# A hybrid diffusion trunk on one core: an output projection over eight full blocks, a fused split of the weights, and unread products in the mixing

## The chip, the core and the metric

The kernel runs on one core of one Trainium2 chip, as one program. The metric is the device time of an execution in microseconds (us), lower is better. Engines are named as in the profile: PE is TensorE's matmul side (PEld its weight loads), DVE is VectorE, ACT is ScalarE, POOL is GpSimd, and SP is the sync engine, whose queue issues all of this kernel's DMAs.

## The reference, cut to what matters

A trunk of two layers runs over 128 context tokens and 256 latent tokens; they are one stream of T = 384 columns, of width 1024. Each layer is a half-step SwiGLU, a token mixing, and a second half-step SwiGLU, each behind an RMS norm with shift, scale and gate from a conditioning vector.

The token mixing projects its input once and runs three head groups side by side:

```
out_a = gqa_attention(a_q, keys_a, vals_a)             # 6 heads of 64: width 384
out_b = rms_norm(gla_bidir(...)) * silu(b_r)           # 4 heads of 64: width 256
out_c = rms_norm(diff_attention(c_q, keys_c, vals_c))  # 4 heads of 96: width 384
out   = concatenate([out_a, out_b, out_c]) @ w_out     # 1024 x 1024
```

Latent tokens read latent and context keys, context tokens only context keys. diff_attention takes the difference of two softmaxes in each head. gla_bidir is linear attention with decays, in both directions. Everything is fp32.

## The kernel before, in words

**Layout.** Activations lie transposed: 128 features on the partitions, the 384 tokens in the columns. A product with a weight is three matmuls (`mm3`): weight and activation are each split into a rounded high part and the rest, and high x high, high x low and low x high are summed in a PSUM bank. `load_split` (L297 to L305) loads a weight tile into one of five raw buffers, rounds it on ACT (L303) and subtracts on DVE (L304); three buffers each for the high and the low part. PE executes its matmuls in the order of its queue.

**Stages.** `ffn` runs 22 blocks of gate and up, then 8 output tiles; beside them, `AdaStream` computes the conditioning vectors with DVE (L254). `mixing` runs named stages in an order written out by hand for each layer (`ORDER`): `wq`, `wk`, `wa`, `wv` and `bv` are projections (`proj_m`), `rq`, `rk` and `ra` norm, rotate and transpose queries and keys on PE, `L0` to `L6` are the levels of the linear attention (in each, `scores` computes 24 small products of 32 rows by 64 columns), `c0` to `c3` are the four differential heads (`c_head`: scores, two softmaxes, transposes, values, sum of squares), `n0` and `n1` norm two heads each, `s0` and `s1` split them, `p0` to `p2` and `o0` to `o2` are the other attention, `go` ends the linear attention. A scheduler interleaves stages on the engines where data and buffers allow, so instructions of several stages alternate in the trace.

**Products in fp32.** Those outside `mm3` (scores, values, sums of squares) take both operands in fp32; the trace shows each as two matmul passes. Transposes are one pass each.

**The output projection** at the end of `mixing` runs over 8 output tiles. The mixed features come in nine blocks, in the order `KORD`: three of the `a` group and two of the `b` group with 128 rows each, and four of the `c` group with 96 rows each, one for every head. The weight `wo` of a tile is loaded in two parts, of five and four blocks; the 96-row blocks are padded to 128 in memory.

**PSUM.** Three banks `mm`, three `ax`, and the banks `ada` and `both` that stages take in turn.

Of the kernel before, what the change touches and what calls it, by code (L numbers as in the profile page):

```python
# [17 lines left out]
P = 128  # L18
D = 1024
KT = 8  # L20
# [42 lines left out]
ORDER = (  # L63
    ("ha br bq hb bk wq bv lg rq de wk st L0 rk L1 cx wa wv L2 c0 L3 c1 L4 c2 ra L5 L6 n0 s0 c3 n1 p0 ax "
     "s1 go o0 p1 p2 o1 o2").split(),
    ("br ha hb bq bk bv lg L0 wq rq wk de L1 st rk L2 wa cx wv L3 c0 ra L4 c1 c2 L5 c3 n0 L6 p0 ax "
     "go o0 p1 s0 p2 o1 n1 s1 o2").split(),
)
KORD = (
    ("c0 c1 c2 c3 b0 b1 a0 a1 a2").split(),  # L70
    ("a0 b0 b1 c0 c1 a1 c2 c3 a2").split(),
)
# [9 lines left out]
def _build(ctx, tc, nc, I, O):  # L82
# [214 lines left out]
    def load_split(src, cols=WCOL):  # L297
        raw = wp.tile([P, WCOL], F32, tag="wraw", bufs=NRAW, name="wraw")
        di = nc.sync.dma_start(out=raw[:, :cols] if len(src.shape) == 2 else
                               raw[:, :cols].rearrange("p (j c) -> p j c", j=src.shape[1]), in_=src)  # L300
        hi = wp.tile([P, WCOL], F32R, tag="whi", bufs=3, name="whi")
        lo = wp.tile([P, WCOL], F32R, tag="wlo", bufs=3, name="wlo")
        S.activation(out=hi[:, :cols], in_=raw[:, :cols], func=AF.Copy)  # L303
        vi = V.tensor_tensor(out=lo[:, :cols], in0=raw[:, :cols], in1=hi[:, :cols].bitcast(F32), op=ALU.subtract)  # L304
        return hi, lo, vi, di  # L305

    def mm3(ps, lh, ll, rh, rl, start, stop):
        PE.matmul(ps, lhsT=lh, rhs=rh, start=start, stop=False)  # L308
        PE.matmul(ps, lhsT=lh, rhs=rl, start=False, stop=False)  # L309
        return PE.matmul(ps, lhsT=ll, rhs=rh, start=False, stop=stop)  # L310

    def newton(pool, ss, n, scale, parts, tag):
# [248 lines left out]
    def mixing(l, us, acc, nxt):  # L561
        turn["own"] = {"mm": ("both",), "ax": ("ada",)}
        r_ = make_rstd(acc)
        with tc.tile_pool(name=f"mix{l}", bufs=1) as mp:
# [3 lines left out]
            def t512(n=512):  # L568
                return mt([P, 512], "t5", N512)[:, :n]


            kta = mt([P, T], "kta")
# [36 lines left out]
            def proj_m(name, n, kper):  # L609
                ps = [mmps()[:, :n] for _ in range(3)]  # L610
# [126 lines left out]
            def a_probs(i):  # L737

                pts = [mt([P, 3, LAT], "pt", NPT), mt([P, 3, LAT], *(("e", 3) if i else ("pt", NPT)))]
                for t in range(2):  # L740
                    pp = [mmps()[:, :T] for _ in range(2)]
                    for g in range(2):
                        r = slice(64 * g, 64 * g + 64)
                        PE.matmul(pp[g], lhsT=qta[r, i, (t + 1) * P:(t + 2) * P], rhs=kta[r, :], start=True, stop=True)
                    for g, (p, rs) in enumerate(map(smax, pp)):
                        S.activation(out=p, in_=p, func=AF.Copy, scale=rs)
                        to_pt(p.rearrange("p (a b) -> p a b", a=3), 3, pts[g][:, :, t * P:(t + 1) * P])
                return pts

            def a_out(i, pts):  # L750
# [12 lines left out]
                V.tensor_tensor(out=lo, in0=po, in1=hi.bitcast(F32), op=ALU.subtract)  # L763
                moa.append((P, hi, lo))

# [17 lines left out]
            def c_head(h, oc, osq, pss):  # L783
                pt = mt([P, 3, LAT], "pt", NPT)
                for t in range(2):
                    pp = [(mmps if PMM[4] else axps)()[:, :T] for _ in range(2)]
                    for m in range(2):
                        r = slice(64 * m, 64 * m + 64)
                        PE.matmul(pp[m], lhsT=qtc[r, h, (t + 1) * P:(t + 2) * P], rhs=ktc[r, h, 0:T],  # L789
                                  start=True, stop=True)  # L790
                    (p0, r0), (p1, r1) = map(smax, pp)
# [20 lines left out]
            def c_first(j):  # L812
                cp[j] = mt([P, 2, T], "oc", 2)[:96], mt([P, 2, T], "pt", NPT)[:96], []
                c_next(j, 0)

            def c_next(j, i):
                oc, osq, pss = cp[j]
                c_head(2 * j + i, oc[:, i, :], osq[:, i, :], pss)

            def c_norm(j):  # L820
                oc, osq, pss = cp[j]
                r = rsq_bcast(mp, pss, T, 1.0 / 96, 96, "c", osq, osq)
                V.scalar_tensor_tensor(out=oc, in0=oc, scalar=gco[:96], in1=r, op0=ALU.mult, op1=ALU.mult)

            def c_split(j):
                oc = cp[j][0]
                for i in range(2):
                    hi = hp.tile([P, TW], F32R, tag="h", name="chi")[:96, :T]
                    S.activation(out=hi, in_=oc[:, i, :], func=AF.Copy)
                    lo = hp.tile([P, TW], F32R, tag="h", name="clo")[:96, :T]  # L830
                    V.tensor_tensor(out=lo, in0=oc[:, i, :], in1=hi.bitcast(F32), op=ALU.subtract)
                    moc.append((96, hi, lo))

# [60 lines left out]

            def scores(q, k, h, cross):
                ps = (mmps if PMM[10] else axps)()[:, :192].rearrange("p (c t) -> p c t", c=3)
                r = slice(32 * h, 32 * h + 32)
                for c in range(3):
                    for f in range(2):
                        fq = 1 - f if cross else f  # L900
                        PE.matmul(ps[64 * f:64 * f + 64, c, :], lhsT=k[r, c * P + 64 * f:c * P + 64 * f + 64],  # L901
                                  rhs=q[r, c * P + 64 * fq:c * P + 64 * fq + 64], start=True, stop=True)
                return ps

            def gla_diag():
                for h in range(4):
                    ps = scores(qk[:, 0, :], qk[:, 1, :], h, False)
                    V.tensor_tensor(out=sd[h // 2][:, h % 2], in0=ps, in1=two_i[:, None, :].to_broadcast([P, 3, 64]),
                                    op=ALU.mult)

            def gla_level(li):
# [33 lines left out]
            def gla_out():  # L945
# [31 lines left out]
                for i in range(2):  # L977
# [3 lines left out]
                    V.tensor_tensor(out=lo, in0=ot[:, i, :], in1=hi.bitcast(F32), op=ALU.subtract)  # L981
                    mob.append((P, hi, lo))

            sv = {}

# [4 lines left out]
            def a_rope():  # L990
                xa, ra = sv["a"]
                for t in range(3):
# [28 lines left out]
            def c_rope(w):  # L1021
                xc, rc = sv[w]
                for t in range(3):
# [9 lines left out]
                    ps = (mmps if PMM[13] else axps)()  # L1033
                    for h in range(4):
                        PE.transpose(ps[:, h * P:(h + 1) * P], pad[:, 2 * h:2 * h + 2, :].rearrange("p a b -> p (a b)"),
# [33 lines left out]
            turn["own"] = {"mm": ("both",), "ax": ()}  # L1069
            mo = [{"a": moa, "b": mob, "c": moc}[n[0]][int(n[1])] for n in KORD[l]]  # L1070
            acc = new_acc()
            us = []
            for m in range(KT):
                ps = mmps()[:, :T]
                for k0, k1 in ((0, 5), (5, 9)):
                    w = load_split(I["wo"][l, m][:, k0 * P:k1 * P], (k1 - k0) * P)
                    for k in range(k0, k1):
                        c = (k - k0) * P
                        n, hi, lo = mo[k]
                        mm3(ps, w[0][:n, c:c + P], w[1][:n, c:c + P], hi, lo, k == 0, k == 8)  # L1080
                end_tile(l, 1, m, ps, acc, nxt, None)
# [137 lines left out]
```

## Time and profile before

| what | value |
|---|---|
| median of three runs | 1598.27 us (1590.26 to 1601.04) |
| profiled execution, its own time | 1599.75 us |
| its span, first to last instruction | 1597.9 us |
| PE busy | 1563.3 us (98%) |
| DVE busy | 1229.3 us (77%) |
| ACT busy | 738.8 us (46%) |
| mean granted clock of TensorE | 0.980 |

A row of a window gives each engine's busy time in that stretch with the number of its instructions, then the granted clock as a share of the full one, the DMA engines' share and what they moved. Durations of single matmuls overlap, since they are pipelined: the distance between the starts of two is the pace. A bracket at the end of a timeline row is the idle time before the instruction and who ended it.

### The profile page before, as it was taken

What the parts mean: (1) busy time and instruction counts of PE and PEld (TensorE: products, weight loads), DVE (VectorE), ACT (ScalarE), POOL (GpSimd) and SP (SyncE); (2) the same over time, 40 slices, a digit from 0 to 9 for tenths busy, and PEclk for the clock granted to TensorE, in tenths of its full rate; (3) what the DMA queues carried; (4) which work ended last, traced back from release to release, by engine and by line L of the source; (5) the groups of instructions that cost most, each with busy time, mean ns of one, the idle gap of its engine ahead of it and who ended that gap; (6) DMA issues with size and microseconds to landing.
All of it is one profiled execution on the core that took longest, in us unless ns stands there. A gap on an engine that the chain in (4) does not pass through costs nothing.

```text
span 1597.9 us, 25055 instructions
## 1 busy us (share of the span) xinstructions
PE 1563.3 (98%) x9370; PEld 1464.0 (92%) x9370; DVE 1229.3 (77%) x2294; ACT 738.8 (46%) x1444; POOL 196.2 (12%) x239
## 2 busy tenths in 40 slices
PE   7999999999999999999999999999999999999999
PEld 5999999997558999999999999999875699999999
DVE  4799999888766888898968889667787767666532
ACT  4544433365466544443344444335546754444321
POOL 1211130030000211111001111102000011111100
PEclk9999999999789999999999999999898999999999
DMA  9677778542104566666666666543321064443441
GB/s 330 231 229 229 226 225 261 165 122 83 45 1 140 168 197 202 201 192 207 204 213 197 210 197 195 174 144 96 113 77 39 1 230 144 143 137 130 120 143 57
DMA packets 83230, 256.38 MB, mean 160 GB/s; under 512 B 10978, under 2 KB 19746, under 8 KB 82722
## 3 DMA queue, kind: packets, MB, share of 16 engines
q1 hardware_dynamic: 83108, 254.78, 50.3%
q8 instruction: 74, 1.21, 0.3%
q14 instruction: 48, 0.39, 0.1%
HBM read 251.99 MB, written 2.75 MB: 159 GB/s over the span
## 4 chain that ended last, share of the span: by engine, by line
PE 90%; DVE 6%; ACT 2%; issue 1%; DMA 1%; POOL 1%; SPq 0%; DVEq 0%; ACTq 0%; POOLq 0%
PE mm L308 20%; PE mm L310 20%; PE mm L309 20%; PE both L308 7%; PE both L309 7%; PE both L310 7%; PE mm L789 1%; DVE wlo L304 1%; PE ax L803 1%; PE ax L901 1%; PE ax L721 1%; DVE junk L254 1%; PE ax L807 0%; DVE ht L397 0%; PE ax L758 0%
## 5 line engine op out<-in xcount | busy, mean ns | idle before, releaser
L303 ACT ACTIVATE whi<-wraw 128x1024 fp32r<-128x1024 f32 (+4 forms) x358 | 348.4, 975 | 461.2 <-PE mm L309 259.1
L304 DVE TENSOR_TENSOR wlo<-wraw,whi 128x1024 fp32r<-128x1024 f32 (+4 forms) x358 | 451.8, 1264 | 131.0 <-ACT whi L303 129.0
L310 PE MATMUL mm<-h,wlo 128*128 128x386 f32 x1096 | 373.3, 341 | 2.5 <-DVE wlo L304 2.5
L308 PE MATMUL mm<-h,whi 128*128 128x386 f32 x1096 | 372.8, 341 | 2.6 <-POOL h L367 1.4
L309 PE MATMUL mm<-h,whi 128*128 128x386 f32 x1096 | 372.5, 340 | 0.0
L254 DVE SCALAR_TENSOR_TENSOR junk<-araw,cb 128x1024 f32<-128x1024 f32 x256 | 312.3, 1220 | 0.8
L310 PEld LDWEIGHTS mm<-h,wlo 128*128 128x128 f32 x1096 | 208.0, 190 | 4.2 <-DVE wlo L304 3.5
L308 PEld LDWEIGHTS mm<-h,whi 128*128 128x128 f32 x1096 | 207.6, 190 | 4.6 <-ACT whi L303 1.7
L309 PEld LDWEIGHTS mm<-h,whi 128*128 128x128 f32 x1096 | 207.6, 189 | 1.6 <-issue 0.7
L477 POOL TENSOR_TENSOR alo<-s,ahi 128x384 fp32r<-128x384 f32 x88 | 115.5, 1314 | 641.5 <-ACT ahi L475 614.9
L309 PE MATMUL mm<-alo,whi 128*128 128x384 f32 x528 | 177.9, 337 | 0.0
L310 PE MATMUL mm<-ahi,wlo 128*128 128x384 f32 x528 | 177.9, 337 | 0.0
L308 PE MATMUL mm<-ahi,whi 128*128 128x384 f32 x528 | 177.9, 337 | 0.0
L308 PE MATMUL both<-h,whi 128*128 128x386 f32 x360 | 122.5, 340 | 0.0
L309 PE MATMUL both<-h,whi 128*128 128x386 f32 x360 | 122.1, 339 | 0.0
L310 PE MATMUL both<-h,wlo 128*128 128x386 f32 x360 | 122.0, 339 | 0.0
L475 ACT ACTIVATE ahi<-s 128x384 fp32r<-128x384 f32 x88 | 46.3, 526 | 129.4 <-DVE s L472 129.3
L309 PEld LDWEIGHTS mm<-alo,whi 128*128 128x128 f32 x528 | 99.2, 188 | 0.0
L310 PEld LDWEIGHTS mm<-ahi,wlo 128*128 128x128 f32 x528 | 99.2, 188 | 0.0
L308 PEld LDWEIGHTS mm<-ahi,whi 128*128 128x128 f32 x528 | 99.2, 188 | 0.0
L469 DVE TENSOR_TENSOR u<-mm,rstd 128x384 f32<-128x384 f32 x66 | 36.6, 554 | 60.8 <-PE mm L310 60.8
L467 ACT ACTIVATE s<-s,bc 128x128 f32<-128x128 f32 (+1 forms) x176 | 70.7, 449 | 8.0 <-ACT bc L418 0.7
(365 smaller groups left out, 2446.7 us busy)
## 6 DMA issues: line engine op xcount, KB each, us to landing
wraw<-in_wgu SPq DMA_DIRECT2D x170, 512.0 KB, 4.2
araw<-in_w_adat SPq DMA_DIRECT2D x128, 512.0 KB, 4.0
wraw<-in_wd SPq DMA_DIRECT2D x64, 512.0 KB, 4.2
wraw<-in_wd SPq DMA_DIRECT2D x32, 384.0 KB, 3.5
araw<-in_w SPq DMA_DIRECT2D x16, 512.0 KB, 5.6
wraw<-in_wo SPq DMA_DIRECT2D x16, 320.0 KB, 3.0
wraw<-in_wit SPq DMA_DIRECT2D x8, 512.0 KB, 3.4
wraw<-in_wa SPq DMA_DIRECT2D x8, 512.0 KB, 3.6
```

Source lines behind the costliest of these rows:

```text
L254: V.scalar_tensor_tensor(out=junk, in0=w, scalar=1.0, in1=self.cb[:, c, :], op0=ALU.mult, op1=ALU.mult, accum_out=self.acc[:, f, c:c + 1])
L303: S.activation(out=hi[:, :cols], in_=raw[:, :cols], func=AF.Copy)
L304: vi = V.tensor_tensor(out=lo[:, :cols], in0=raw[:, :cols], in1=hi[:, :cols].bitcast(F32), op=ALU.subtract)
L308: PE.matmul(ps, lhsT=lh, rhs=rh, start=start, stop=False)
L309: PE.matmul(ps, lhsT=lh, rhs=rl, start=False, stop=False)
L310: return PE.matmul(ps, lhsT=ll, rhs=rh, start=False, stop=stop)
L467: S.activation(out=s[:, a:b], in_=s[:, a:b], func=AF.Silu, bias=bg[:, c:c + 1])
L469: vi = V.tensor_tensor(out=u, in0=pu[:, :T], in1=r, op=ALU.mult)
L475: S.activation(out=hi, in_=s, func=AF.Copy)
L477: G.tensor_tensor(out=lo, in0=s, in1=hi.bitcast(F32), op=ALU.subtract)
L721: pi = PE.transpose(ps[:, i * P:(i + 1) * P], p[:, i, :], ident)
L789: PE.matmul(pp[m], lhsT=qtc[r, h, (t + 1) * P:(t + 2) * P], rhs=ktc[r, h, 0:T], start=True, stop=True)
```

## The change

**The output projection over eight blocks.** Head 3 of the `c` group has no block of its own any more. Its 96 rows fill the rows 96 to 127 of the blocks of heads 0, 1 and 2, 32 rows each, so that eight blocks have 128 rows. `c_norm(1)` writes these rows with three instructions of 32 rows; `c_split(0)` now needs `c_norm(1)`, and `ORDER` moves `s0` behind `n1` in layer 0 and `n1` forward in layer 1. Each part of `wo` has four blocks; the part with the head blocks is loaded by three DMAs (rows 0 to 95, the gathered rows, and the last rows of the one other block).

**The low part of a weight** is computed by `scalar_tensor_tensor` (times 1.0, minus the high part) instead of `tensor_tensor`, on the same operands.

**33 unread products in each mixing.** `warm` issues n products of a 128 x 128 matrix of ones with the identity, in fp32, into columns of a PSUM bank that nobody reads: 4 ahead of the first `proj_m`, 8 ahead of the scores of head 0, one behind the scores of every second head in `gla_diag` and the levels 0 to 2 (8), one ahead of each group of transposes in `a_rope` and `c_rope` (9), 4 ahead of the output projection. The scores of the `a` group and of the other `c` heads get none.

```diff
-    ("ha br bq hb bk wq bv lg rq de wk st L0 rk L1 cx wa wv L2 c0 L3 c1 L4 c2 ra L5 L6 n0 s0 c3 n1 p0 ax "
-     "s1 go o0 p1 p2 o1 o2").split(),
+    ("ha br bq hb bk wq bv lg rq de wk st L0 rk L1 cx wa wv L2 c0 L3 c1 L4 c2 ra L5 L6 n0 c3 n1 p0 ax "
+     "s0 s1 go o0 p1 p2 o1 o2").split(),
...
-     "go o0 p1 s0 p2 o1 n1 s1 o2").split(),
+     "go n1 o0 p1 s0 p2 s1 o1 o2").split(),
...
-    ("c0 c1 c2 c3 b0 b1 a0 a1 a2").split(),
-    ("a0 b0 b1 c0 c1 a1 c2 c3 a2").split(),
+    ("c0 c1 c2 b0 b1 a0 a1 a2 c3").split(),
+    ("a0 b0 b1 a1 c0 c1 c2 a2 c3").split(),
...
-        vi = V.tensor_tensor(out=lo[:, :cols], in0=raw[:, :cols], in1=hi[:, :cols].bitcast(F32), op=ALU.subtract)
+        vi = V.scalar_tensor_tensor(out=lo[:, :cols], in0=raw[:, :cols], scalar=1.0, in1=hi[:, :cols].bitcast(F32),
+                                    op0=ALU.mult, op1=ALU.subtract)
...
+    def warm(ps, n, c=384):
+
+        for _ in range(n):
+            PE.matmul(ps[:, c:c + P], lhsT=ones, rhs=ident, start=True, stop=True)
...
+                ps = [mmps() for _ in range(3)]
+                if not sv.setdefault("pm", 0):
+                    warm(ps[0], 4, 0)
...
+                    pp = [(mmps if PMM[4] else axps)() for _ in range(2)]
+                    if h == t == 0:
+                        warm(pp[0], 8)
...
+                n = 2 - j
+                V.scalar_tensor_tensor(out=oc[:96, :n], in0=oc[:96, :n], scalar=gco[:96], in1=r[:, :n],
+                                       op0=ALU.mult, op1=ALU.mult)
+                if j:
+
+                    for i in range(3):
+                        q = slice(32 * i, 32 * i + 32)
+                        V.scalar_tensor_tensor(out=cp[i // 2][0][96:P, i % 2, :], in0=oc[q, 1, :], scalar=gco[q],
+                                               in1=r[q, 1, :], op0=ALU.mult, op1=ALU.mult)
...
+                if h % 2 and fill:
+                    warm(bk, 1)
...
-                    ps = scores(e[:, 0, :], e[:, 1, :], h, li == 0)
+                    ps = scores(e[:, 0, :], e[:, 1, :], h, li == 0, li < 3)
...
                     ps = (mmps if PMM[13] else axps)()
+                    warm(ps, 1)
                     for i in range(4):
                         PE.transpose(ps[:, i * P:(i + 1) * P], xr[:, i * P:(i + 1) * P], ident)
...
+                parts = [(slice(0, 96), slice(0, (k1 - k0) * P), w[0:96, k0 * P:k1 * P]),
+                         (slice(96, P), slice(b, b + 3 * P),
+                          w[0:96, KT * P:(KT + 1) * P].rearrange("(j p) c -> p j c", j=3))]
+                for k in range(k0, k1):
+                    if not kc <= k < kc + 3:
+                        parts.append((slice(96, P), slice((k - k0) * P, (k - k0 + 1) * P), w[96:P, k * P:(k + 1) * P]))
...
-                for k0, k1 in ((0, 5), (5, 9)):
-                    w = load_split(I["wo"][l, m][:, k0 * P:k1 * P], (k1 - k0) * P)
+                if m == 0:
+                    warm(ps, 4)
+                ps = ps[:, :T]
+                for k0, k1 in ((0, 4), (4, 8)):
+                    w = load_split(wo_parts(I["wo"][l, m], k0, k1), (k1 - k0) * P)
```

## Rows read from the trace of the kernel before

**Rows 1.** The page: granted clock in 40 slices, and the chain that ended last.

```profile
PEclk9999999999789999999999999999898999999999
...
PE 90%; DVE 6%; ACT 2%; issue 1%; DMA 1%; POOL 1%; SPq 0%; DVEq 0%; ACTq 0%; POOLq 0%
```

**Rows 2.** Windows: both mixings, and a stretch of layer 0's output projection.

```profile
311.00:535.00 224.00, 217.02 (x1453) 172.91 (x1452) 169.88 (x433) 134.87 (x303) 28.27 (x40) 0.92 0.29 92
1091.00:1315.00 224.00, 212.56 (x1449) 171.34 (x1448) 169.97 (x428) 132.56 (x298) 25.00 (x34) 0.93 0.29 90
502.00:532.00 30.00, 30.00 (x173) 30.00 (x172) 18.29 (x36) 17.23 (x27) 2.98 (x9) 1.00 0.77 261
```

**Rows 3.** Windows: stretches that were granted half the clock, sum over all eight.

```profile
387.30:390.70 3.40, 3.40 (x17) 2.89 (x16) 3.05 (x7) 1.75 (x11) 0.00 (x0) 0.51 0.46 155
421.40:448.80 27.40, 26.93 (x112) 13.70 (x110) 15.17 (x46) 14.37 (x37) 0.00 (x0) 0.50 0.00 1
...
1128.00:1134.80 6.80, 6.80 (x33) 6.25 (x31) 4.62 (x15) 4.00 (x11) 0.00 (x0) 0.50 0.03 11
...
1213.40:1227.00 13.60, 13.60 (x42) 6.66 (x42) 7.26 (x23) 8.01 (x21) 0.00 (x0) 0.50 0.00 0
...
sum 64.80, PE 64.33 PEld 40.86 DVE 39.56 ACT 35.15 POOL 0.00; mean PE 8.04 PEld 5.11 DVE 4.95 ACT 4.39 POOL 0.00
```

**Rows 4.** Windows: the stretches just ahead of three of the clock's falls.

```profile
418.50:421.40 2.90, 0.75 (x3) 0.49 (x4) 2.85 (x9) 1.48 (x5) 0.00 (x0) 1.00 0.38 114
...
1115.00:1117.80 2.80, 0.92 (x7) 0.76 (x6) 2.69 (x6) 2.80 (x6) 0.99 (x1) 1.00 0.00 0
1125.20:1128.00 2.80, 2.80 (x43) 1.70 (x41) 1.11 (x3) 2.79 (x5) 0.00 (x0) 1.00 0.54 173
```

**Rows 5.** Timeline: second scaling, first projection matmul; a split's DVE half (ns min/median/max).

```profile
477.10 1.00 DVE L823 SCALAR_TENSOR_TENSOR oc<-oc,sp,pt 96x768 f32<-96x768 f32 x1
...
487.91 0.44 PE L308 MATMUL mm<-chi,whi 96*128 96x384 f32 x1
...
L831 DVE TENSOR_TENSOR clo<-oc,chi x8: 543/551/555, 459.3 to 1280.8; 96x384 fp32r<-96x384 f32 x8
```

**Rows 6.** Loads of the projection's weight: us to landing; ns of an issue.

```profile
wraw<-in_wo SPq DMA_DIRECT2D x16, 320.0 KB, 3.0
...
L299 SPq DMA_DIRECT2D wraw<-in_wo x32: 327/328/340, 385.9 to 1297.8; - x32
```

**Rows 7.** Timeline of DVE and POOL, twice; who waited for L304 (us, times).

```profile
225.45 1.22 DVE L254 SCALAR_TENSOR_TENSOR junk<-araw,cb 128x1024 f32<-128x1024 f32 x1
...
226.17 1.37 POOL L477 TENSOR_TENSOR alo<-s,ahi 128x384 fp32r<-128x384 f32 x1 [7.72 <-ACT ahi L475]
...
226.71 1.92 DVE L254 SCALAR_TENSOR_TENSOR junk<-araw,cb 128x1024 f32<-128x1024 f32 x1
...
563.06 1.37 POOL L477 TENSOR_TENSOR alo<-s,ahi 128x384 fp32r<-128x384 f32 x1 [7.88 <-ACT ahi L475]
...
563.49 2.02 DVE L304 TENSOR_TENSOR wlo<-wraw,whi 128x1024 fp32r<-128x1024 f32 x1
...
  PE mm L310: 2.5, 3
```

**Rows 8.** Timeline of PE, layer 1: the context scores of all four heads.

```profile
1188.61 1.71 PE L775 MATMUL ax<-ktc,qtc 64*128 64x128 f32 x16
```

**Rows 9.** Timeline of PE, layer 0: scores of the second head.

```profile
420.65 1.96 PE L789 MATMUL mm<-ktc,qtc 64*128 64x384 f32 x4 [2.46 <-ACT p L697]
```

**Rows 10.** Timeline of PE: L807, each head's last product, layers 0, 1.

```profile
436.39 1.59 PE L807 MATMUL ax<-pt,cst 96*96 96x384 f32 x2
...
448.75 0.90 PE L807 MATMUL ax<-pt,cst 96*96 96x384 f32 x2
...
1233.73 0.89 PE L807 MATMUL ax<-pt,cst 96*96 96x384 f32 x2
...
1240.75 0.89 PE L807 MATMUL ax<-pt,cst 96*96 96x384 f32 x2
```

More of the change, by code (lines that the diff above doesn't have):

```diff
@@ L298, in load_split @@
         raw = wp.tile([P, WCOL], F32, tag="wraw", bufs=NRAW, name="wraw")
-        di = nc.sync.dma_start(out=raw[:, :cols] if len(src.shape) == 2 else
-                               raw[:, :cols].rearrange("p (j c) -> p j c", j=src.shape[1]), in_=src)
+        for rows, cs, part in (src if isinstance(src, list) else [(slice(0, P), slice(0, cols), src)]):
+            dst = raw[rows, cs]
+            if len(part.shape) == 3:
+                dst = dst.rearrange("p (j c) -> p j c", j=part.shape[1])
+            di = nc.sync.dma_start(out=dst, in_=part)
         hi = wp.tile([P, WCOL], F32R, tag="whi", bufs=3, name="whi")
@@ L569, in t512 @@
                 return mt([P, 512], "t5", N512)[:, :n]
+            sv = {}
             kta = mt([P, T], "kta")
@@ L609, in proj_m @@
             def proj_m(name, n, kper):
-                ps = [mmps()[:, :n] for _ in range(3)]
+                ps = [mmps() for _ in range(3)]
+                if not sv.setdefault("pm", 0):
+                    warm(ps[0], 4, 0)
+                sv["pm"] += 1
+                ps = [p[:, :n] for p in ps]
                 for k0 in range(0, KT, kper):
@@ L740, in a_probs @@
                 for t in range(2):
-                    pp = [mmps()[:, :T] for _ in range(2)]
+                    pp = [mmps() for _ in range(2)]
                     for g in range(2):
                         r = slice(64 * g, 64 * g + 64)
-                        PE.matmul(pp[g], lhsT=qta[r, i, (t + 1) * P:(t + 2) * P], rhs=kta[r, :], start=True, stop=True)
-                    for g, (p, rs) in enumerate(map(smax, pp)):
+                        PE.matmul(pp[g][:, :T], lhsT=qta[r, i, (t + 1) * P:(t + 2) * P], rhs=kta[r, :], start=True,
+                                  stop=True)
+                    for g, (p, rs) in enumerate(smax(p[:, :T]) for p in pp):
                         S.activation(out=p, in_=p, func=AF.Copy, scale=rs)
@@ L763, in a_out @@
                 V.tensor_tensor(out=lo, in0=po, in1=hi.bitcast(F32), op=ALU.subtract)
-                moa.append((P, hi, lo))
+                moa.append((hi, lo))
             ptc_ = []
@@ L785, in c_head @@
                 for t in range(2):
-                    pp = [(mmps if PMM[4] else axps)()[:, :T] for _ in range(2)]
+                    pp = [(mmps if PMM[4] else axps)() for _ in range(2)]
+                    if h == t == 0:
+                        warm(pp[0], 8)
                     for m in range(2):
                         r = slice(64 * m, 64 * m + 64)
-                        PE.matmul(pp[m], lhsT=qtc[r, h, (t + 1) * P:(t + 2) * P], rhs=ktc[r, h, 0:T],
+                        PE.matmul(pp[m][:, :T], lhsT=qtc[r, h, (t + 1) * P:(t + 2) * P], rhs=ktc[r, h, 0:T],
                                   start=True, stop=True)
+                    pp = [p[:, :T] for p in pp]
                     (p0, r0), (p1, r1) = map(smax, pp)
@@ L812, in c_first @@
             def c_first(j):
-                cp[j] = mt([P, 2, T], "oc", 2)[:96], mt([P, 2, T], "pt", NPT)[:96], []
+                cp[j] = mt([P, 2, T], "oc", 2), mt([P, 2, T], "pt", NPT)[:96], []
                 c_next(j, 0)
@@ L817, in c_next @@
                 oc, osq, pss = cp[j]
-                c_head(2 * j + i, oc[:, i, :], osq[:, i, :], pss)
+                c_head(2 * j + i, oc[:96, i, :], osq[:, i, :], pss)
             def c_norm(j):
@@ L822, in c_norm @@
                 r = rsq_bcast(mp, pss, T, 1.0 / 96, 96, "c", osq, osq)
-                V.scalar_tensor_tensor(out=oc, in0=oc, scalar=gco[:96], in1=r, op0=ALU.mult, op1=ALU.mult)
-            def c_split(j):
[L826 to L832, printed above, removed]
+                n = 2 - j
[6 more added lines that the diff above has]
+                                               in1=r[q, 1, :], op0=ALU.mult, op1=ALU.mult)
+            def c_split(j):
+                for i in range(2 - j):
+                    oc = cp[j][0][:, i, :]
+                    hi = hp.tile([P, TW], F32R, tag="h", name="chi")[:, :T]
+                    S.activation(out=hi, in_=oc, func=AF.Copy)
+                    lo = hp.tile([P, TW], F32R, tag="h", name="clo")[:, :T]
+                    V.tensor_tensor(out=lo, in0=oc, in1=hi.bitcast(F32), op=ALU.subtract)
+                    moc.append((hi, lo))
             bv = mt([P, 3, 256], "bv")
@@ L893, in mixing, with scores @@
             sc = [mt([P, 2, 3, P], f"sc{i}") for i in range(2)]
-            def scores(q, k, h, cross):
-                ps = (mmps if PMM[10] else axps)()[:, :192].rearrange("p (c t) -> p c t", c=3)
+            def scores(q, k, h, cross, fill):
+                bk = (mmps if PMM[10] else axps)()
+                ps = bk[:, :192].rearrange("p (c t) -> p c t", c=3)
                 r = slice(32 * h, 32 * h + 32)
@@ L906, in gla_diag @@
                 for h in range(4):
-                    ps = scores(qk[:, 0, :], qk[:, 1, :], h, False)
+                    ps = scores(qk[:, 0, :], qk[:, 1, :], h, False, True)
                     V.tensor_tensor(out=sd[h // 2][:, h % 2], in0=ps, in1=two_i[:, None, :].to_broadcast([P, 3, 64]),
@@ L981, in gla_out @@
                     V.tensor_tensor(out=lo, in0=ot[:, i, :], in1=hi.bitcast(F32), op=ALU.subtract)
-                    mob.append((P, hi, lo))
-            sv = {}
+                    mob.append((hi, lo))
             def a_proj():
@@ L1033, in c_rope @@
                     ps = (mmps if PMM[13] else axps)()
+                    warm(ps, 1)
                     for h in range(4):
@@ L1069, in mixing, with wo_parts @@
             turn["own"] = {"mm": ("both",), "ax": ()}
-            mo = [{"a": moa, "b": mob, "c": moc}[n[0]][int(n[1])] for n in KORD[l]]
+            mo = [{"a": moa, "b": mob, "c": moc}[n[0]][int(n[1])] for n in KORD[l][:KT]]
+            kc = KORD[l].index("c0")
+            def wo_parts(w, k0, k1):
+                if not k0 <= kc < k1:
+                    return w[:, k0 * P:k1 * P]
+                b = (kc - k0) * P
+                parts = [(slice(0, 96), slice(0, (k1 - k0) * P), w[0:96, k0 * P:k1 * P]),
[4 more added lines that the diff above has]
+                        parts.append((slice(96, P), slice((k - k0) * P, (k - k0 + 1) * P), w[96:P, k * P:(k + 1) * P]))
+                return parts
             acc = new_acc()
@@ L1073, in mixing @@
             for m in range(KT):
-                ps = mmps()[:, :T]
-                for k0, k1 in ((0, 5), (5, 9)):
-                    w = load_split(I["wo"][l, m][:, k0 * P:k1 * P], (k1 - k0) * P)
+                ps = mmps()
+                if m == 0:
[3 more added lines that the diff above has]
+                    w = load_split(wo_parts(I["wo"][l, m], k0, k1), (k1 - k0) * P)
                     for k in range(k0, k1):
                         c = (k - k0) * P
-                        n, hi, lo = mo[k]
-                        mm3(ps, w[0][:n, c:c + P], w[1][:n, c:c + P], hi, lo, k == 0, k == 8)
+                        hi, lo = mo[k]
+                        mm3(ps, w[0][:, c:c + P], w[1][:, c:c + P], hi, lo, k == 0, k == KT - 1)
                 end_tile(l, 1, m, ps, acc, nxt, None)
```

## The prediction

> **What bounds the kernel now.** I read the page first. The chain of work that ended last is 90% TensorE (PE), and the clock line is at full speed but for two places, around slices 11 to 13 and 29 to 32 of 40 [rows 1]. A chain of PE work gets shorter in two ways only: less PE work, or the same work at a higher clock.
>
> The windows by stage say where. Both token mixings take 224 us and have a mean granted clock of 0.92 and 0.93; the output projection at their end runs 173 matmuls in 30 us with PE busy throughout, and VectorE (DVE) at 18 us is no limit there [rows 2]. Cut along the clock's falls, eight stretches, 64.8 us in all, were granted 0.50, that is 1.2 GHz where the rest has 2.4 GHz, and PE is busy in 64.3 of the 64.8 us [rows 3]. Four of them, each 3.4 us and PE busy throughout, are not shown: at 479.5, 1117.8, 1179.2 and 1271.4 us. The two long ones, 27.4 and 13.6 us, lie in the differential-attention heads (c0 to c2 of the stage order).
>
> What PE did ahead of the falls is of two kinds. Before 421.4 and 1117.8 us it waited (busy 0.75 of 2.90 us and 0.92 of 2.80 us). Before 1128.0 us it was busy for the whole 2.80 us, with 43 small instructions: 32-row score products of the linear attention and one 32-row product of the decays [rows 4]. So PE lost the clock there without a wait, on products of few rows.
>
> **The change, part by part.**
>
> Eight blocks in place of nine: each of 8 output tiles in each of 2 layers loses 3 matmuls, 48 in all. The projection's pace is 30.00/173 = 0.173 us per matmul [rows 2], so 48 x 0.173 = 8.3 us, if every one stands on the path. Not every one does: the projection's first matmuls start at 487.91 us, amid the last softmaxes [rows 5], and fill gaps of PE. Six matmuls a layer (one block of the two tiles begun early) may have cost nothing before: 12 x 0.173 = 2.1 us. Bounds 6.2 and 8.3; I take 7.3 off.
>
> Its cover: the part of head 3 that fills the three head blocks is now written by three 32-row DVE instructions beside a half-sized one, for one of 1.00 us [rows 5]; at the 0.55 us that a 384-wide DVE operation takes there, 2.2 us for 1.0, while one split (two instructions) goes. The old scaling ended at 478.1 us, the first matmul that needs it starts at 487.91 [rows 5]: some 9 us hide 1.2 us. Without that cover it would be 1.2 us a layer. The move of the first split behind the second scaling lies under the same cover.
>
> Its loads: each tile's two transfers become four, so 32 more issues of 0.328 us on SyncE's queue, 5 us a layer; a weight's conversion on ScalarE waits for three landings, not one. Queued behind it on ScalarE are the squares of the finished tiles and the next conversions; DVE's low part and then PE wait for it. Five raw buffers run ahead, and a landing takes 3.0 us [rows 6] against 24 x 0.173 = 4.2 us per tile. Taken as 0; if the cover were gone, about 3 us once per layer.
>
> The fused low part: a plain subtraction of 1024 columns that starts while GpSimd (POOL) runs is held until POOL is done; one of the 77 such, of 258, stands in the rows, at 2.02 us. The fused form with two SBUF operands is in the trace too, in the conditioning stream: 1.22 us, and 1.92 us when it starts behind the same POOL line [rows 7]. So I take 0. If it escaped the hold, DVE would gain 77 x 0.8 = 62 us, but the longest that PE waited for low parts is 2.5 us in total at one line of the three-product helper [rows 7], so 5 us in two: bounds 0 and 5.
>
> The 66 unread products (33 a layer): none is in the trace. The nearest row is the score product of 128 columns, two passes each, 16 passes in 1.71 us: 0.107 us a pass, 0.214 us a product at 2.4 GHz [rows 8]. All 66 on the path: 14.1 us, or 28.2 us at 1.2 GHz; all in waits: 0. Site by site: the 4 ahead of the first wide projection meet a busy PE in layer 0 (0.85 us) and a coming wait in layer 1 [rows 4] (0). Of the 16 among the scores, the 18 ahead of the transposes and the 8 ahead of the output projection I put half on the path: 1.7 + 1.9 + 0.85. The 8 ahead of the first head stand before its scores, and the softmax behind them starts later; but PE then waits 2.46 us for that softmax's buffers [rows 9], so of 1.7 us I count 0.6 in each layer. Sum 6.5 us.
>
> What the clock gives back. The heads first. At 1.2 GHz two successive head ends are 448.75 - 436.39 = 12.4 us apart, at 2.4 GHz 1240.75 - 1233.73 = 7.0 [rows 10]. On 41.0 us of low heads the ratio 0.57 gives 17.8 us; DVE's 15.2 and ScalarE's 8.0 busy us, which can't shrink, give the same limit (12.2 + 5.6) [rows 3]. If the clock falls later among the heads all the same, part of it is lost, since nothing is added beside most of the attention scores: bounds 0 and 17.8; I take 12. Four shorter stretches, 17.0 us (387.3, 1117.8, 1128.0, 1179.2), have products in or just ahead of them. Half, 8.5 us, is the most; DVE is busy 3.05 of 3.40 us in the first [rows 3], so I take 5.5. The falls at 479.5 and 1271.4 have none near: 0.
>
> Sum: -7.3 - 12 - 5.5 + 6.5 = -18.3 us. The profiled execution took 1599.75 us (span 1597.9); the median of three runs, 1598.27, is 1.5 us lower. 1599.75 - 18.3 - 1.5 = 1580 us.
>
> By the Trainium skill, "TensorE: Matmul & The Clock Gate", section "Why this matters for your kernels", throughput drops come from PE-idle gaps between matmul bursts. The trace agrees for two of the three falls shown and differs for the third: PE had no idle gap before 1128.0 us [rows 4]. By the page alone, the products in busy places would be cost without return; this is the fourth case below.
>
> **Rivals.**
>
> Second case: every product falls into a wait, and the heads come down to DVE's limit: -8.3 - 17.8 - 8.5 + 3 = -31.6 us, 1567 us. For it: DVE and ScalarE have room in the low stretches (15.2 and 14.4 of 27.4 us) [rows 3]. Against it: the softmaxes alternate between engines.
>
> Third case: the heads still fall, some microseconds later, and stay low as before: -7.3 - 5.5 + 6.5 = -6.3 us, 1592 us. For it: in the 27.4 us PE is busy in 26.9 and stays at 1.2 GHz [rows 3]; once low, these half-height products don't bring it back.
>
> Fourth case: only waits let the clock fall. Then of the short stretches only 1117.8 us gains (1.7 us at most, I take 1): -7.3 - 12 - 1 + 6.5 = -13.8 us, 1584.5 us.
>
> Fifth case: the products don't hold the clock anywhere: -7.3 + 6.5 to 14.1, so 1597 to 1605 us.
>
> Slower: the eight products ahead of the first head and those among the scores stand in PE's in-order queue ahead of work that others wait for, at 1.2 GHz. All 66 on the path at 0.43 us: 28.2 - 6.2 = +22 us, 1620 us. It decides from the point where the low time stays near 65 us and no more than a fifth of the products falls into waits (16 + 6.2 = 22.2 of 28.2 us). Against it: PE waits 2.46 us at the very place of the eight [rows 9].
>
> **How the numbers follow.** Within 1% of the median, about 16 us, this kernel's runs tell little from no change: the bounds are 1582.3 and 1614.3. Forecast 0.45 (own range 1572 to 1588, two thirds of it under 1582.3, so 0.30); second case 0.20, faster; third 0.20, same; fourth 0.05, of which 0.02 faster; fifth 0.05, same; slower 0.05. Faster 0.52, same 0.43, slower 0.05. The range 1567 to 1596 leaves out about 0.08 below (the second case's lower part, and a fused form that escapes the hold) and the 0.10 of the last two above.
>
> **What would show it.** Projection: 24 matmuls a tile, pace still 0.173 us, and the mixing's end some 3.6 us shorter in each layer by it. Low stretches: about 20 us in place of 64.8, with 3.4 us left at the two places without products; the gap between head ends near 7 us in both layers. Products: 132 passes near 0.107 us apart, mostly where PE waited. Fused form: the low part still near 2.0 us behind POOL. The forecast is wrong if the clock falls after the first head's products as it did before, if the wider conversions wait for their third landing, or if the changed order puts other work ahead of the softmaxes.

## The result and the profile after

The changed kernel took 1607.22 us (median of 10 runs, 1600.14 to 1611.19), the kernel before 1595.84 us in runs beside it: a ratio of 1.0069, 95% interval 1.0043 to 1.0095, 0.7% slower, which lies inside the prediction's own bounds for no change (1% either way). The forecast was 1580 us, the range 1567 to 1596. Both sign and size were wrong. The profiled execution took 1611.19 us, its span is 1609.4 us, its mean granted clock 0.979.

The page of the kernel after, granted clock in 40 slices and the shares of the chain that ended last, against [rows 1]:

```profile
PEclk9999999999978999999999999999998999999999
...
PE 91%; DVE 5%; ACT 2%; DMA 1%; issue 1%; POOL 0%; SPq 0%; DVEq 0%; ACTq 0%
```

PE still sets the end, and the two dips of the clock are still there. The windows of both mixings (from the end of the first half-step to the last matmul of the projection) and 30 us of layer 0's projection, against [rows 2]:

```profile
311.70:544.40 232.70, 227.13 (x1482) 178.31 (x1481) 169.25 (x431) 132.46 (x299) 26.05 (x34) 0.90 0.27 83
1104.10:1326.50 222.40, 214.72 (x1482) 171.76 (x1482) 171.19 (x431) 131.81 (x299) 24.59 (x34) 0.95 0.29 88
514.40:544.40 30.00, 30.00 (x171) 29.61 (x170) 19.62 (x40) 18.48 (x30) 3.02 (x8) 1.00 0.79 259
```

The loss of this execution lies in layer 0: between the same two events the mixing took 221.6 us before. Layer 1 took 222.7 us before and 222.4 after. Every stretch with half the clock, and the 2.8 us ahead of the longest, against [rows 3, 4]:

```profile
387.90:394.70 6.80, 6.80 (x47) 5.85 (x48) 5.04 (x14) 3.03 (x14) 0.00 (x0) 0.50 0.14 39
435.70:439.10 3.40, 3.40 (x18) 2.04 (x18) 1.56 (x6) 2.20 (x7) 0.00 (x0) 0.51 0.00 0
459.50:497.00 37.50, 35.77 (x124) 18.35 (x124) 15.03 (x44) 18.34 (x51) 2.21 (x6) 0.50 0.00 1
1138.80:1145.60 6.80, 6.80 (x35) 6.20 (x31) 4.44 (x15) 3.59 (x10) 0.00 (x0) 0.50 0.01 3
1227.50:1241.20 13.70, 13.26 (x42) 6.97 (x42) 5.35 (x17) 7.31 (x20) 0.00 (x0) 0.50 0.00 0
sum 68.20, PE 66.04 PEld 39.41 DVE 31.43 ACT 34.48 POOL 2.21; mean PE 13.21 PEld 7.88 DVE 6.29 ACT 6.90 POOL 0.44
...
456.70:459.50 2.80, 2.78 (x85) 2.30 (x80) 2.47 (x9) 0.16 (x2) 0.18 (x1) 1.00 0.02 6
```

68.2 us of low clock in place of 64.8. The 27.4 us in layer 0's heads shrank to 3.4 us, but the clock fell again at 459.5 us, behind 2.80 us in which PE was busy for 2.78, most of it with 32-row score products:

```profile
456.88 0.68 PE L929 MATMUL ax<-e 32*64 32x64 f32 x22
```

It stayed low for 37.5 us while the a heads (ordinary attention), the end of the last c head and small products of the linear attention ran. Head ends (each head's last product), against [rows 10]:

```profile
439.98 0.89 PE L826 MATMUL ax<-pt,cst 96*96 96x384 f32 x2
446.69 0.89 PE L826 MATMUL ax<-pt,cst 96*96 96x384 f32 x2
453.48 0.89 PE L826 MATMUL ax<-pt,cst 96*96 96x384 f32 x2
466.33 1.59 PE L826 MATMUL ax<-pt,cst 96*96 96x384 f32 x2
```

Three heads end 6.7 and 6.8 us apart, as forecast for the full clock; the last falls into the low stretch, 12.9 us later. Layer 0's scores and the eight products ahead of the first head (L319 is the products' line), where [rows 9] have a wait ahead of the second head's scores, and PE's waits that follow:

```profile
420.92 0.39 PE L929 MATMUL ax<-e 32*64 32x64 f32 x6
...
421.59 0.49 PE L319 MATMUL ada<-cst 128*128 128x128 f32 x2
422.01 0.74 PE L929 MATMUL ax<-e 32*64 32x64 f32 x24
422.68 0.49 PE L319 MATMUL ax<-cst 128*128 128x128 f32 x2
423.01 1.95 PE L319 MATMUL mm<-cst 128*128 128x128 f32 x16
424.89 0.92 PE L807 MATMUL mm<-ktc,qtc 64*128 64x384 f32 x4
...
427.15 0.91 PE L807 MATMUL mm<-ktc,qtc 64*128 64x384 f32 x2 [0.70 <-ACT p L712]
428.55 0.91 PE L807 MATMUL mm<-ktc,qtc 64*128 64x384 f32 x2 [0.48 <-ACT p L712]
...
431.19 0.55 PE L736 MATMUL ax<-cst,p 128*128 128x128 f32 x3 [0.61 <-DVE p L816]
...
433.38 0.91 PE L807 MATMUL mm<-ktc,qtc 64*128 64x384 f32 x2 [0.58 <-ACT p L712]
```

The eight are 16 passes, 1.88 us from the first to the head's first score: 0.235 us a product. PE does not wait right ahead of them or right behind them. Behind the first head's scores it waits again, 0.70, 0.48, 0.61 and 0.58 us, together 2.37 us where [rows 9] have 2.46 us. The single product between two sets of 32-row scores takes 0.42 us, from its start to that of the next score (421.59 to 422.01).

### The profile page after: what moved, and what is told of

Its sections match the earlier page's. It is cut to its first block, busy times and chain, and to the rows that moved or that the text cites. A ratio compares the mean times of both kernels' runs of the same rounds, so it can differ in the third digit from the quotient of the medians.

```text
span 1609.4 us, 25287 instructions
## 1 busy us (share of the span) xinstructions
PE 1579.1 (98%) x9454; PEld 1473.5 (92%) x9454; DVE 1232.4 (77%) x2298; ACT 736.3 (46%) x1442; POOL 197.6 (12%) x239
## 4 chain that ended last, share of the span: by engine, by line
PE 91%; DVE 5%; ACT 2%; DMA 1%; issue 1%; POOL 0%; SPq 0%; DVEq 0%; ACTq 0%
PE mm L312 20%; PE mm L313 20%; PE mm L314 20%; PE both L314 7%; PE both L312 7%; PE both L313 7%; DVE wlo L307 1%; PE ax L929 1%; PE mm L807 1%; PE ax L736 1%; PE ax L822 1%; PE mm L759 1%; DVE junk L254 1%; PE ada L929 0%; DMA araw<-in_w 0%
## 5 line engine op out<-in xcount | busy, mean ns | idle before, releaser
L306 ACT ACTIVATE whi<-wraw 128x1024 fp32r<-128x1024 f32 (+3 forms) x358 | 346.4, 970 | 458.8 <-PE mm L313 258.4
L307 DVE SCALAR_TENSOR_TENSOR wlo<-wraw,whi 128x1024 fp32r<-128x1024 f32 (+3 forms) x358 | 450.5, 1261 | 127.4 <-ACT whi L306 124.2
```

Of the source, the lines that this page charges most:

```text
L307: vi = V.scalar_tensor_tensor(out=lo[:, :cols], in0=raw[:, :cols], scalar=1.0, in1=hi[:, :cols].bitcast(F32), op0=ALU.mult, op1=ALU.subtract)
```

## The experiments

**How the runs are read.** The runs of one kernel differ by up to 22 us, and the difference goes with the granted clock that each run lists. For a run of T us at mean clock c, the low time is 2 x (1 - c) x T, since the low level is half. Over 183 runs (35 of the kernel before, 10 of the one after, 138 of the twelve versions below), each kernel taken about its own mean, one us of low time costs 0.406 us (standard error 0.008; 1.3 us of scatter is left). Taken singly, the 14 kernels give 0.28 to 0.48. A us at half clock can cost at most 0.5 us of PE work. "At full clock" below is a kernel's mean time less 0.406 x its mean low time; it is worked out, not measured. Each ratio is to runs of the kernel before beside the same version; in the four sets of such runs beside the versions (110 runs) that kernel's median is 1591.9 to 1597.5 us, and at full clock it comes out at 1573.7 to 1574.3.

| kernel | products, both layers | median us | ratio to before, 95% interval | mean low time | at full clock |
|---|---|---|---|---|---|
| before (35 runs) | 0 | 1594.2 | | 52.4 | 1573.7 |
| after | 66 | 1607.2 | 1.0069 [1.0043, 1.0095] | 57.5 | 1582.9 |
| after, none | 0 | 1588.7 | 0.9953 [0.9926, 0.9980] | 51.6 | 1566.1 |
| before, with them | 66 | 1602.1 | 1.0048 [1.0022, 1.0075] | 42.5 | 1585.6 |
| before, fused form | 0 | 1590.6 | 1.0005 [0.9979, 1.0032] | 48.4 | 1573.8 |
| fill all | 134 | 1596.1 | 1.0010 [0.9987, 1.0033] | 13.8 | 1590.5 |
| thin products | 66 | 1608.3 | 1.0090 [1.0060, 1.0119] | 62.7 | 1582.0 |
| doubled | 132 | 1600.2 | 1.0044 [1.0016, 1.0072] | 22.2 | 1591.6 |
| a side filled too | 106 | 1602.4 | 1.0043 [1.0015, 1.0071] | 37.7 | 1586.7 |
| 8 in a wait | 16 | 1588.4 | 0.9971 [0.9938, 1.0003] | 47.2 | 1569.1 |
| c heads only | 44 | 1586.6 | 0.9962 [0.9936, 0.9987] | 33.6 | 1574.6 |
| 40 ahead of a projection | 80 | 1598.0 | 1.0024 [1.0000, 1.0048] | 41.5 | 1580.5 |
| heads and a side | 84 | 1593.6 | 1.0027 [0.9995, 1.0058] | 23.0 | 1587.8 |
| 16 in the waits | 32 | 1587.9 | 0.9958 [0.9936, 0.9979] | 36.8 | 1573.2 |

**Parts of the change.** First the changed kernel without its products:

```diff
 def warm(ps, n, c=384):
-    for _ in range(n):
-        PE.matmul(ps[:, c:c + P], lhsT=ones, rhs=ident, start=True, stop=True)
+    return
```

> The changed kernel without the 33 products per mixing: 8 blocks, the new order and the fused low part stay; only products that nobody reads are left out. Theory 1 (the blocks save their 6 to 8 us, the products lose about 18 us): 1588 us, ratio to the kernel before 0.993 to 0.997, low-clock time near the 64.8 us of before. Theory 2 (the new order of steps and blocks slows the attention stage, the products are harmless): 1600 us or more, ratio 1.003 or more, with the heads no shorter than before. Theory 3 (the products cost only their own time on TensorE, some 14 us for 66): ratio 0.996 to 0.999.

Its windows over the two mixings:

```profile
313.70:525.60 211.90, 205.73 (x1416) 162.89 (x1416) 167.89 (x431) 131.90 (x299) 26.26 (x34) 0.94 0.30 91
1085.30:1305.50 220.20, 208.50 (x1417) 165.66 (x1416) 170.07 (x431) 132.09 (x299) 24.83 (x34) 0.93 0.29 88
```

Theory 1's time, low time unchanged. The interval overlaps theory 3's ratio too, so this run does not tell those two apart. Theory 2 falls: blocks, order and fused form together gain 7.6 us at full clock. The whole loss, 18.5 us between the medians, comes with the products. PE's waits in these windows sum to 6.17 + 11.70 = 17.9 us without products and to 5.57 + 7.68 = 13.3 us with them: the products used up 4.6 us of waits.

The two profiled executions can be set side by side without the fit of all runs. PE is busy 27.6 us longer with the products (441.85 against 414.23 us in these windows). Low time in the mixings is 68.2 us with them and 54.8 without (the sum of the version's four low stretches there):

```profile
sum 54.80, PE 53.57 PEld 32.91 DVE 32.71 ACT 28.16 POOL 0.00; mean PE 13.39 PEld 8.23 DVE 8.18 ACT 7.04 POOL 0.00
```

If half of the 13.4 us more is put down to the clock, 20.9 us of PE's work are left; less the 4.6 us of waits this is an estimate of 16.3 us, close to the 16.8 us of the table. That is more than 66 products at 0.235 us (15.5 us). A part of it shows at the 32-row scores. Without products:

```profile
416.80 0.39 PE L928 MATMUL ax<-e 32*64 32x64 f32 x6
...
417.82 0.92 PE L806 MATMUL mm<-ktc,qtc 64*128 64x384 f32 x4
```

48 passes of scores take 1.02 us up to the first head's scores. With two products among them, the same 48 passes take 2.09 us up to the eight (420.92 to 423.01), 0.53 us more for each product.

Then the products alone, put into the kernel before: `warm(...)` at the same places, 9 blocks, old order, plain subtraction.

> The kernel before plus the 33 unread products per mixing at the same places, nothing else: 9 blocks, old order, plain subtraction. Theory 1: ratio 1.009 to 1.013 (+14 to +20 us), the clock falling again behind the last score products of a layer and staying low through the stage of the a heads. Theory 2: ratio 0.999 to 1.002. Theory 3: +14 us (1.009), whatever the clock does; the two are told apart by the low-clock time, which theory 1 has at or above 65 us, and theory 3 below 50 us.

+7.9 us in the median, less than theory 1 said: the low time is lower than before, not higher. At full clock they cost 11.9 us; theory 3 said 14, and its low time (below 50 us) is right. In its profiled run the clock fell among layer 0's heads all the same, at 428.8 us for 23.9 us and at 456.1 us for 10.2 us.

The fused form alone (slices left out):

```diff
-vi = V.tensor_tensor(out=lo, in0=raw, in1=hi, op=ALU.subtract)
+vi = V.scalar_tensor_tensor(out=lo, in0=raw, scalar=1.0, in1=hi, op0=ALU.mult, op1=ALU.subtract)
```

> The kernel before with the fused low part alone. All theories: ratio 0.999 to 1.001, mean duration of the fused low part within 10 ns of the 1264 ns that the subtraction takes. A ratio above 1.003 would put a part of the loss on this form.

No difference that the runs can show. In the kernel after, the form is still held when it starts behind POOL, as in [rows 7]:

```profile
565.46 1.38 POOL L486 TENSOR_TENSOR alo<-s,ahi 128x384 fp32r<-128x384 f32 x1 [4.22 <-ACT ahi L484]
565.89 2.03 DVE L307 SCALAR_TENSOR_TENSOR wlo<-wraw,whi 128x1024 fp32r<-128x1024 f32 x1
```

**Is it their own time or the clock?** The same products with the same 128 columns of data, on a corner of the array:

```diff
-PE.matmul(ps[:, c:c + P], lhsT=ones, rhs=ident, start=True, stop=True)
+PE.matmul(ps[:32, c:c + P], lhsT=ones[:32, :32], rhs=ident[:32, :], start=True, stop=True)
```

> The changed kernel with each unread product on 32 rows and 32 columns of TensorE's array in place of 128 and 128, over the same 128 columns of data, so as long as before but small. Theory A (a product costs its own 0.214 us on the path, 14 us for 66, and the clock is a separate matter): 1600 to 1608 us, no faster than the changed kernel, with low-clock time near that of the kernel without products (a mean of 52 us). Theory B (the loss comes from what the full products do to the clock): 1588 to 1593 us, as without products.

The products' line, ns min/median/max, in the kernel after and then with thin products:

```profile
L319 PE MATMUL mm<-cst x64: 271/275/377, 329.6 to 1284.8; 128*128 128x128 f32 x64
```

```profile
L319 PE MATMUL mm<-cst x64: 267/268/292, 330.3 to 1278.0; 32*32 32x128 f32 x64
```

A pass lasts as long, and the kernel is as slow as the changed one: theory A. It costs 15.9 us at full clock over the version without products (the full ones 16.8). Its low time, 62.7 us, is above the 52 us that theory A expected. Theory B would have had 1588 to 1593 us.

The price by itself, 40 products where PE never waits (`warm(ps[0], 40, 0)` ahead of the first wide projection, the others out):

> The changed kernel with 40 products ahead of the first wide projection of each mixing and no others: 80 in all, in a place where the clock is at full speed and TensorE is 99% busy. Theory A: 80 x 0.214 to 0.247 us = 17 to 20 us on top of the 1588.7 us without products: 1605 to 1609 us, low-clock time unchanged (a mean near 52 us). If VectorE, 83 to 90% busy beside that stretch, sets its end: 1589 to 1598 us.

PE's timeline, layer 0:

```profile
330.42 0.34 PE L314 MATMUL mm<-h,wlo 128*128 128x386 f32 x1
330.60 9.10 PE L319 MATMUL mm<-cst 128*128 128x128 f32 x80
339.45 0.42 PE L312 MATMUL mm<-whi,h 128*128 128x384 f32 x1
```

8.85 us for 40, 0.221 us each, with no gap. Counted from the end of the first half-step, the context scores of the c heads began 8.3 us later than without them in layer 0 and 6.5 us in layer 1. At full clock the 80 cost 14.4 us, 0.18 each: short of the 17 us of theory A, and the median, 1598.0 us, stands at the top of the rival's range. So most of a product's own time is paid even beside a busy DVE, but not all of it.

**More products.** Beside all scores: 2 ahead of each other score pair of the c heads and of each of the a heads, and one behind every second score set in all seven levels (shortened):

```diff
-                    if h == t == 0:
-                        warm(pp[0], 8)
+                    warm(pp[0], 8 if h == t == 0 else 2)     # c heads; a heads: warm(pp[0], 2)
-scores(e[:, 0, :], e[:, 1, :], h, li == 0, li < 3)
+scores(e[:, 0, :], e[:, 1, :], h, li == 0, True)
```

> The changed kernel with 34 more unread products per mixing, beside the score products of the c heads and a heads that had none, and behind the score products of all seven levels. Theory 1: the clock holds through the heads and the stage of the a heads, low-clock time 35 us or less (it was 68.2), and the time falls below that of the changed kernel, 1590 to 1602 us. Theory 3 (a product costs its 0.214 us on the path and the clock matters little): 1607 + 68 x 0.214 = 1622 us.

The clock holds, 13.8 us of low time, and the time falls 11 us under the changed kernel with 68 more products. That is theory 1's range. But at full clock 134 products cost 24.4 us, 0.18 each, so the cost is near theory 3's; each theory was half right.

Each product of the change twice (`range(2 * n)`):

> The changed kernel with each unread product made twice (66 per mixing, same places). Theory A: 14 us more at the same low-clock time, less 0.4 us for each us of low-clock time that goes: 1609 to 1621 us. Theory C (products stand mostly in waits, the loss is the fall at 459.5 us): 1600 to 1608 us, as the second product of a place would then also lie in a wait.

Not as theory A had it. Low time drops from 57.5 to 22.2 us, and the second 66 cost 8.7 us at full clock, half of the first. The time lies in theory C's range. Over the 12 runs the granted clock was 0.988 to 0.999. In the profiled one two products at a place hold the clock where one did not; its page shows no dip in any slice:

```profile
PEclk9999999999999999999999999999999999999999
```

Only where the clock of the changed kernel fell at 459.5 us: 2 ahead of each pair of a-head scores, one behind every second score set of the last four levels, the rest as changed.

> The changed kernel with 20 more products per mixing, only in the stretch where its clock fell at 459.5 us: 2 ahead of each pair of a-head scores, one behind every second score set of the last four levels. Theory A with the moved fall: own time of 40 products 5 to 8.5 us, low-clock time down from a mean of 57 us to 15 to 25 us, which gives back 13 to 16 us: 1597 to 1604 us. If the clock has another cause than the small products of that stretch, low-clock time stays above 45 us and the time rises to 1611 us or more.

The time is as expected, the low time is not: 37.7 us on average. In the profiled run the long stretch at 459.5 us is gone (3.4 us at 464.6), but 10.2 us each at 389.6 and 433.9, 13.7 us at 1219.0 and shorter ones remain.

**Fewer, in better places.** Only 8 a layer, behind the scores of the first c head, where PE had waited (shortened):

```diff
-                    if h == t == 0:
-                        warm(pp[0], 8)
 ...
+                    if h == 0 and t == 1:
+                        warm(pp[1], 8)          # all others left out
```

> The changed kernel with only 8 products per mixing, moved behind the scores of the first c head, where TensorE stood idle for 2.2 us in the kernel without products; all others left out. Theory A: in a wait they cost nothing, and what they hold of the clock is gain: 1578 to 1587 us, not above the 1588.7 us without products; low-clock time 20 to 45 us. If products cost even there: 1592 us.

PE's timeline, first without products, then with the 8:

```profile
418.90 0.48 PE L806 MATMUL mm<-ktc,qtc 64*128 64x384 f32 x1
421.58 1.64 PE L806 MATMUL mm<-ktc,qtc 64*128 64x384 f32 x4 [2.20 <-ACT p L711]
```

```profile
418.42 2.05 PE L320 MATMUL mm<-cst 128*128 128x128 f32 x16
420.69 0.91 PE L806 MATMUL mm<-ktc,qtc 64*128 64x384 f32 x2 [0.22 <-ACT p L713]
423.46 0.52 PE L737 MATMUL ax<-cst,p 128*128 128x128 f32 x3 [1.86 <-DVE p L817]
```

The wait is filled (2.20 to 0.22 us), a second one of 1.86 us follows, and the clock falls at 424.9 us. Low time went down by 4 us, and there is no gain: 1588.4 against 1588.7 us. That they cost nothing is not shown either: at full clock the 16 cost 3 us, which the timeline does not explain. With 16 a layer (`warm(pp[1], 16)`):

> The changed kernel with 16 products per mixing behind the scores of the first c head and no others, twice as many as the run that put 8 there. With 8, TensorE's first wait (2.2 us) was filled, a second one of 1.86 us followed behind the next scores, and the clock fell at 424.9 us all the same. Theory A: 10 of the 16 lie ahead of the first probability transposes and use up both waits at no cost, 6 lie behind them at 0.21 to 0.25 us each, 2.5 to 3 us for both layers; if the filled second wait keeps the clock, low-clock time goes from a mean of 47 us to 20 to 30 us, 7 to 11 us back: 1579 to 1585 us. If the fall only comes later, in the other heads: low-clock time above 40 us and 1589 to 1592 us.

1587.9 us. Low time falls to 36.8 us, at full clock the 32 cost 7.1 us: what the clock gives, 6.0 us, does not quite pay for them. The clock still fell at 424.9 us, for 3.4 us, behind a wait of 2.54 us that ten of the 16 left open:

```profile
425.02 0.87 PE L737 MATMUL ax<-cst,p 128*128 128x128 f32 x3 [2.54 <-DVE p L817]
```

The 8 in the wait and 2 ahead of each other score pair of the c heads:

> The changed kernel with 22 products per mixing, all in the c heads: 8 in the wait behind the first head's scores and 2 ahead of each of the other seven score pairs; none in the wide projections, the ropes, the levels or ahead of the output projection. Theory A (own time on the path, 0.4 us back for each us of low-clock time that goes): 28 of the 44 on the path cost 3 to 6.5 us; low-clock time from a mean of 52 us to 20 to 30 us gives back 9 to 13 us: 1579 to 1585 us, under the 1588.7 us without products. If the fall only moves on to the a heads: low-clock time 40 us or more, 1587 to 1592 us.

1586.6 us, just above the range, with the low time a little above it too. The same and the a side:

> The changed kernel with 42 products per mixing, all from the first c head on: those of the run with c heads only, 2 ahead of each pair of a-head scores and one behind every second score set of the last four levels; none ahead of that. Theory A: 6 to 14 us of own time, low-clock time down to a mean of 5 to 15 us gives back 15 to 19 us: 1577 to 1587 us, the best of the versions so far. If the clock needs the products of the wide projections and ropes too: low-clock time above 30 us, 1590 us or more.

The low time is 23.0 us, but the 84 cost 21.7 us at full clock, 0.26 each, and the time is no better than before. No version with products is measurably faster than the changed kernel without them (0.9953).

## Why the prediction was wrong, point by point

At full clock and with the mean low times of the table, the result is a sum of three terms: -7.6 us for blocks, order and fused form, +16.8 us for the products, +0.406 x (57.5 - 52.4) = +2.1 us for the clock. Together +11.3 us, the measured difference of the means (1606.2 - 1594.9). It has to come out so, as "at full clock" is defined by it: the sum divides the difference and is no check of it. The prediction had -7.3 (blocks, with 0 for the rest), +6.5 and -17.5.

**What bounds the kernel:** right, PE's share of the chain is 91%.

**Blocks:** right as far as the runs show, 7.6 us for 7.3. The new order and the fused form are in it, and no run has the eight blocks alone. The pace is 30.00/171 = 0.175 us [rows 2].

**Cover of the scaling:** right. The four scalings (one of head 2, three of head 3) take 2.49 us in the place of 1.00 [rows 5], and end at 477.63 us, 26 us ahead of the first projection matmul (504.21 us):

```profile
475.12 0.61 DVE L843 SCALAR_TENSOR_TENSOR oc<-oc,sp,pt 96x384 f32<-96x384 f32 x1
475.75 1.88 DVE L849 SCALAR_TENSOR_TENSOR oc<-oc,sp,pt 32x384 f32<-32x384 f32 x3
```

**Loads:** right as far as the trace shows. The pieces land in 2.5 to 2.8 us; a median issue takes 0.394 us, not 0.328 [rows 6]; ScalarE waited once for a landing, 3.6 us, and PE's pace did not change:

```profile
wraw<-in_wo SPq DMA_DIRECT2D x16, 256.0 KB, 2.8
wraw<-in_wo SPq DMA_DIRECT2D x16, 192.0 KB, 2.6
wraw<-in_wo SPq DMA_DIRECT2D x16, 48.0 KB, 2.5
wraw<-in_wo SPq DMA_DIRECT2D x16, 16.0 KB, 2.6
```

**Fused form:** right, 0.1 us.

**Products:** wrong, the first of the two failed steps: +6.5 us, where the 66 cost 11.9 us in the old order and 16.8 us in the new one, 0.18 and 0.25 us each. Two things in it failed. The first is the share on the path: "I put half on the path", and of the eight ahead of the first head "0.6 in each layer". In [rows 2] PE's waits in both mixings sum to 18.4 us, in the version without products to 17.9 us, and with the products 13.3 us are left. So only 4.6 us of waits were used up. The wait of 2.46 us [rows 9], which was to take the eight, comes after the first head's scores; products ahead of the scores push the scores, the softmax and the wait back together, and 2.37 us of waits stand there again.

The second is the price. 0.214 us is near what products in a row take (0.221 and 0.235 us). It is not what a single one takes among the 32-row scores, where 16 of the 66 stand: two of them lengthened that stretch by 0.53 us each. So the 14.1 us that stood as the upper bound at 2.4 GHz was none: the new order's 16.8 us lie above it. Why the 66 cost 4.9 us less in the old order stays open.

**The clock:** wrong, the second failed step: 12 us for the heads ("I take 12") and 5.5 us for the four shorter stretches ("so I take 5.5"), together -17.5, measured as +2.1. Its conversion was good: 17.5 us for about 45 us less of low time is 0.39 per us, and 0.406 is measured. The low time did not go away. In the profiled run of the kernel after, layer 0's heads had 3.4 us of low time in place of 27.4, and the fall came at the next place without products, where it lasted 37.5 us. In that of the products alone the heads fell as before (23.9 us), so one profiled run does not show that the products held them. "If the clock falls later among the heads all the same" was in the text, as a bound of one stretch; the third case let the fall come later and last as long as before; that it can move out of the heads and last longer there was not priced. In two versions (all filled, doubled) the products did hold it, at a price that the clock does not pay back.

**The fall at 1128.0 us** [rows 4] was read rightly: PE lost the clock there without a wait, while it ran products of few rows. The fall at 459.5 us is a second, longer case. That the few rows are the cause is not shown; with products added in that stretch, the long fall was gone from the profiled run. By the Trainium skill, "TensorE: Matmul & The Clock Gate", section "Why this matters for your kernels", idle gaps of PE between bursts of matmuls are what makes throughput drop; this case's traces agree for the heads (a wait of 1.86 us ahead of the fall at 424.9 us in the version with 8 in the wait) and differ for 459.5 us (PE busy for 2.78 of 2.80 us).

**The rivals:** nearest is the fifth (products hold the clock nowhere, 1597 to 1605 us), given 0.05; its mean low time was right and its price for the products too small. The slower case had the products at 1.2 GHz; most ran at 2.4 GHz (a median pass of 275 ns among the 64 of the 132 passes listed), and their price there was enough.

## What to carry to other kernels

Before an operation is costed at half because "PE waits somewhere here", add up PE's waits over the whole stage: where it is 95% busy, what is added ahead of it on an in-order queue is paid nearly in full. Its price is taken from the place where it will stand: here 0.22 us in a row of its own kind, 0.53 us among small products. Work that is to keep a clock up must save more low time than it costs: here one us at half clock is worth 0.41 us and one product costs 0.18 to 0.26 us, so a product has to remove about half a us of low time (0.44 to 0.64 us). And a remedy that covers one stretch is judged by the total low time over many runs, not by that stretch, because the fall can move.

## What the runs showed of the hardware

A product of 32 rows, 32 columns of the array and 128 columns of data takes as long as one of 128 by 128 (268 and 275 ns a pass). The granted clock differed between runs of the same kernel by up to 0.016 (0.978 to 0.994 in the one with 8 in a wait), and with it the time by 22 us. Over 14 kernels taken together that relation had a slope of 0.406 us per us of low time, 0.28 to 0.48 in single kernels. One product between two sets of 32-row scores took 0.42 us to the next score's start, against 0.22 us in a row of forty. The clock fell behind 2.80 us in which PE was busy for 2.78, and then stayed at half through 37.5 us in which PE was busy for 35.77.
